# Low parts of the w_up weights: a ScalarE negation and an accumulating DMA in place of a VectorE subtraction

## The chip, the cores and the metric

The kernel runs on one core of one Trainium2 chip. The metric is the time of one execution on the device in microseconds (us); the profile gives the start and duration of every instruction of one such execution.

## What is computed

Two encoder layers on 512 positions of width 1024, all in float32. Cut to what matters here, a layer is

```python
h   = _mixer_sublayer(x, ...)                  # projections, two attention mixers, gates, w_out
x   = _layer_norm(DEEPNORM_ALPHA * x + h, ln1_g[i], ln1_b[i])
mlp = square(relu(x @ w_up[i])) @ w_down[i]    # 1024 -> 4096 -> 1024
ple = sigmoid(x @ w_ple_gate[i] + b_ple_gate[i]) * (p[i] @ w_ple[i])
x   = _layer_norm(DEEPNORM_ALPHA * x + mlp + ple, ln2_g[i], ln2_b[i])
```

The change concerns the weights `w_up` of the MLP.

## The kernel before

Every product of two float32 operands is made of three matmuls: each operand is split into a high part (rounded to the type float32r) and a low part (what is left), and the kernel sums high·high, low·high and high·low (`mm3`, lines 270 to 273). Weights come from HBM in packed sets of 128x1024 elements (512 KB). A set passes through three tiles, each with three buffers: `wst` (the raw weights, loaded by SP in `fetch`), `whi` and `wlo` (made in `prep` by the helper `split`). The helper is two instructions: ScalarE copies with a rounding, VectorE subtracts.

```python
nc.scalar.copy(hi, src)                                               # L225
nc.vector.tensor_tensor(lo, src, hi.bitcast(F32), ALU.subtract)       # L226
```

`weights(key, look, further)` hands out the next set and, before that, lets `ahead` prepare sets up to `look` places further on and fetch up to `further` places. With three buffers, set c+2 takes the buffers of set c-1, so its copy may begin when the product of set c-1 has ended.

The MLP of a layer goes in four quarters q of 1024 hidden channels. A quarter has an up stage and a down stage. The up stage is a loop over eight sets of `w_up`, in the order `UP_ORDER` (m = 0, 4, 1, 5, ...); the text below counts them by the loop index i, as P0 to P7 for their products. Each product is 24 matmuls (`mm3` for eight k) into one PSUM bank of the pool "mm". After each, `dn.hidden` writes the squared ReLU: ScalarE takes `r` (relu, L1016) and the high part (`a11h` L1020 for m < 4, `axh` L1023 otherwise), GpSimd takes `hr` = r·r (L1024), VectorE the low part (L1027, L1029). For m of 4 and more VectorE also forms four combinations `sr` (L1031 to L1033), which ScalarE copies to `smh` (L1034) and VectorE subtracts to `sml` (L1035).

The down stage multiplies these with `w_down` in seven products n of a Strassen-like scheme (`dn.product`, L1051), whose results VectorE adds to `yt` (`gather`, L1070). The sets of `w_down` lie in tiles `raw`; `dn.add` (L1004) sums two of them, and `dn.cut(q, n, c)` splits one by the same helper: the half c = 0 into the pool of `whi` and `wlo`, the half c = 1 into tiles `dhi` and `dlo`. So `w_up` sets and halves of `w_down` share three pairs of buffers. In each quarter the first cuts and adds are issued in the up loop, after P2 and later, and the first sets of the next quarter are prepared in the down stage (`behind`).

TensorE's order of work is the program's own (a manual schedule). On ScalarE, VectorE and GpSimd a scheduler with a time estimate of its own sets the order of the instructions, which the engines then run strictly in that order.

Of the kernel before, what the change touches and what calls it, by code (L numbers as in the profile page):

```python
# [10 lines left out]
F32 = mybir.dt.float32  # L11
F32R = mybir.dt.float32r
I32 = mybir.dt.int32
AF = mybir.ActivationFunctionType
ALU = mybir.AluOpType
# [185 lines left out]
def build(nc, tc, plan, down, xT, pT, wst, vec, sink, cst, outT):  # L201
# [3 lines left out]
    with ctx:  # L205
# [4 lines left out]
        def bank(tag, name):  # L210
            return pp.tile([P, 512], F32, tag=tag, name=name, bufs={"mm": 3, "s": 2, "pt": 2, "o": 1}[tag])
# [12 lines left out]
        def split(hi, lo, src):  # L224
            nc.scalar.copy(hi, src)  # L225
            nc.vector.tensor_tensor(lo, src, hi.bitcast(F32), ALU.subtract)  # L226
# [16 lines left out]
        def prep(c):  # L243
            st, n, cut = fetched.pop(c)
            hi = wp.tile([P, 1024], F32R, tag="whi", name=f"whi{c}")
            lo = wp.tile([P, 1024], F32R, tag="wlo", name=f"wlo{c}")
            for a in range(0, n, cut):
                split(hi[:, a:a + cut], lo[:, a:a + cut], st[:, a:a + cut])
            ready[c] = (hi, lo)

        def ahead(last, further=0):
            while at[1] < len(plan) and at[1] <= max(last, further):
                fetch(at[1])
                at[1] += 1
                if at[1] - 1 <= last:
                    prep(at[2])
                    at[2] += 1
            while at[2] < len(plan) and at[2] <= last:
                prep(at[2])
                at[2] += 1  # L260

        def weights(key, look=LOOK, further=0):
            c = at[0]
            assert plan[c][0] == key, (plan[c][0], key)
            at[0] += 1
            ahead(c + look, c + further)
            return ready.pop(c)

        def mm3(ps, w, i, x, start, stop):
            s = slice(i * P, (i + 1) * P)  # L270
            nc.tensor.matmul(ps, w[0][:, s], x[0], start=start, stop=False)  # L271
            nc.tensor.matmul(ps, w[0][:, s], x[1], start=False, stop=False)  # L272
            nc.tensor.matmul(ps, w[1][:, s], x[0], start=False, stop=stop)  # L273

        def linear(key, xs, ps=None):
            w = weights(key)
            if ps is None:
                ps = bank("mm", "ps_" + "_".join(str(v) for v in key))
            for i, x in enumerate(xs):
                mm3(ps, w, i, x, i == 0, i == len(xs) - 1)  # L280
            return ps
# [527 lines left out]
        class Norm:  # L809
# [87 lines left out]
            def behind(self, ins):  # L897
                tc.add_manual_dep(ins.ins, self.last.ins.name, mybir.DependencyInfo(
                    mybir.DependencyClass.Sync, mybir.DependencyReason.DATA), reason="statistics first")
# [245 lines left out]
        def pool(name, side="left"):  # L1145
            c = ExitStack()
            return c.enter_context(tc.tile_pool(name=name, bufs=1, side=side, reuse_waits="tile")), c.close
# [3 lines left out]
        for l in range(DEPTH):  # L1151
# [50 lines left out]
            for u in range(4):  # L1202
                gs = [gate(l, 1, t, vt, rp) for t in (2 * u, 2 * u + 1)]
                w = weights((l, ("bb", u)))
# [45 lines left out]
            def residual_turned(a):  # L1250
                for d in range(2):
                    tp = bank(("pt", "s")[a % 2], f"yT{l}_{a}_{d}")
                    for i in range(4):
                        nc.tensor.transpose(tp[:, i * P:(i + 1) * P], y[4 * d + i][:, a * P:(a + 1) * P], ident)
                    nc.scalar.copy(dn.y[a][:, d * 512:(d + 1) * 512], tp)
# [3 lines left out]
            with tc.manual_schedule(engines={PE}):  # L1259
                pss = []  # L1260
                for i in range(2):
                    pss.append(linear((l, ("up", 0, UP_ORDER[i])), X))
                    residual_turned(2 * i)
                    residual_turned(2 * i + 1)
                yp_close()
                p0_close()
                hp, hp_close = pool(f"hp{l}", "right")
                dn.hp = hp
                dn.operands()
                for q in range(FQ):  # L1270
                    for i, m in enumerate(UP_ORDER):
                        if not i:
                            dn.load(q)
                        if q or i > 1:
                            w = weights((l, ("up", q, m)), (2, 2, 2, 2, 2, 1, 1, 0)[i], min(3, 7 - i))
                            ps = bank("mm", f"ps_up{l}_{q}_{m}")
                            for k, x in enumerate(X):
                                mm3(ps, w, k, x, k == 0, k == KT - 1)
                        else:
                            ps = pss[i]  # L1280
                        dn.hidden(q, m, ps)
                        if i == 2:
                            dn.cut(q, 0, 1)
                        if q == FQ - 1 and i in (1, 2):
                            dn.spread(i - 1, dn.v[i - 1])
                        if i == 3:
                            dn.add(2, 1)
                            dn.cut(q, 1, 1)
                        if i == 4:
                            dn.add(5, 1)  # L1290
                        if i == 5:
                            dn.cut(q, 0, 0)
                        if i == 6:
                            dn.add(2, 0)
                            dn.add(5, 0)
                            dn.cut(q, 2, 1)
                        if i == 7:
                            dn.cut(q, 1, 0)
                            dn.add(3, 1)
                            dn.cut(q, 3, 1)  # L1300
                            dn.add(6, 1)
                    def behind(n, s):

                        with tc.issue_after(dn.ready.ins):
                            if n < 4:
                                if s:
                                    dn.cut(q, n + 2, 0)
                                    if n in (0, 1):
                                        dn.add((3, 6)[n], 0)
                                elif n:  # L1310
                                    dn.cut(q, n + 3, 1)
                            elif n == 4:
                                if not s:
                                    dn.cut(q, 6, 0)
                            elif s:
                                ahead(at[0] + n - 5, at[0] + 2)
                        if q == FQ - 1 and n == 1:
                            dn.moments(s, 0)

                    for n in range(7 if q < FQ - 1 else 4):  # L1320
                        dn.product(q, n, lambda s: behind(n, s))
                if not last:
                    ph, pl = (qp.tile([P, 2, S], F32R, name=f"p{e}{l + 1}", tag=f"raw11{i}", bufs=1) for i, e in enumerate("hl"))
                    pf = qp.tile([P, 2, S], F32, name=f"pf{l + 1}", tag="raw100", bufs=1)
                    nc.sync.dma_start(pf, pT[l + 1])
            q = FQ - 1
# [78 lines left out]
```

## Time and profile before

| | |
|---|---|
| three runs | 1571.17, 1571.31, 1573.22 us (median 1571.31) |
| the profiled execution, its own time | 1573.54 us |
| its span, first to last instruction | 1571.8 us |
| busy share of TensorE / VectorE / ScalarE / GpSimd | 98% / 69% / 47% / 18% |
| granted TensorE clock, mean | 0.996 of full speed |
| bytes moved, rate over the span | 143.37 MB, 91 GB/s |

The span lies 1.7 us under the execution's own time. A matmul's bar in the profile lasts longer than the distance to the next matmul's start, since matmuls overlap: rates are read from starts. A row of idle time names the instruction that ended it.

### The profile page before, as it was taken

To read this page: it belongs to the slowest core of one execution; us is meant where nothing else is said; L and a number is where in the kernel's file an instruction comes from. 1 tells how busy PE (TensorE), PEld (TensorE's weight loads), DVE (VectorE), ACT (ScalarE), POOL (GpSimd) and SP (SyncE) were. 2 spreads that over 40 slices of the span, in tenths; PEclk is the share of its full clock that TensorE was granted. 3 is DMA by queue.
4 is the path that set the end of the run, shared out by engine and by line. 5 is a ranking of instruction groups with operands and counts; after the bars stand their busy time and mean duration, and the time that the engine had idled before them with its cause. 6 is when DMAs were issued, how large, how long until landed. Compare 5 with 4: busy or idle time off the path is not lost.

```text
span 1571.8 us, 19688 instructions
## 1 busy us (share of the span) xinstructions
PE 1533.4 (98%) x7482; PEld 1254.0 (80%) x7482; DVE 1079.9 (69%) x1759; ACT 741.6 (47%) x1237; POOL 288.4 (18%) x208
## 2 busy tenths in 40 slices
PE   8999999999999999999899999999999999999997
PEld 6777888878888888888677778888887888888886
DVE  6878674454947777686868786744549476777867
ACT  4666554333644443434445665543336444434343
POOL 1010100157111111202000101101572111112020
PEclk9999999999999999999999999999999999999999
DMA  6212122232532414141132112223325324241401
GB/s 216 68 54 67 55 82 85 90 104 77 221 94 69 132 56 151 49 148 41 40 106 68 54 57 66 78 79 99 95 79 206 103 75 128 65 149 46 142 1 54
DMA packets 42736, 143.37 MB, mean 91 GB/s; under 512 B 5136, under 2 KB 7312, under 8 KB 42640
## 3 DMA queue, kind: packets, MB, share of 16 engines
q1 hardware_dynamic: 42064, 142.03, 28.4%
q8 instruction: 59, 0.97, 0.3%
q14 instruction: 37, 0.30, 0.1%
q10 hardware_dynamic: 576, 0.07, 0.0%
HBM read 139.98 MB, written 2.10 MB: 90 GB/s over the span
## 4 chain that ended last, share of the span: by engine, by line
PE 86%; DVE 8%; ACT 3%; issue 2%; DMA 1%; SPq 0%; ACTq 0%; DVEq 0%
PE dn L1051 16%; PE ps_up L273 7%; PE ps_up L272 7%; PE ps_up L271 7%; DVE wlo L226 2%; PE sa L399 1%; PE pta L377 1%; PE ps_start L271 1%; PE ps_start L272 1%; PE sb L399 1%; PE ps_start L273 1%; PE ya L271 1%; PE ya L273 1%; PE ya L272 1%; PE ps_pg L272 1%
## 5 line engine op out<-in xcount | busy, mean ns | idle before, releaser
L226 DVE TENSOR_TENSOR wlo<-wst,whi 128x1024 fp32r<-128x1024 f32 (+1 forms) x197 | 261.7, 1332 | 184.6 <-ACT whi L225 167.8
L225 ACT CAST whi<-wst 128x1024 fp32r<-128x1024 f32 (+1 forms) x197 | 202.3, 1029 | 352.8 <-PE ps_up L272 106.7
L1024 POOL TENSOR_TENSOR hr<-r 128x512 f32<-128x512 f32 x64 | 102.1, 1595 | 568.5 <-ACT r L1016 568.5
L271 PE MATMUL ps_up<-xhi,whi 128*128 128x512 f32 x480 | 186.9, 389 | 0.0
L273 PE MATMUL ps_up<-xhi,wlo 128*128 128x512 f32 x480 | 186.7, 389 | 0.0
L272 PE MATMUL ps_up<-xlo,whi 128*128 128x512 f32 x480 | 186.7, 389 | 0.0
L225 ACT CAST whi<-raw 128x1024 fp32r<-128x1024 f32 x56 | 58.0, 1052 | 101.4 <-PE ps_up L272 62.0
L272 PEld LDWEIGHTS ps_up<-xlo,whi 128*128 128x128 f32 x480 | 90.1, 188 | 18.8
L271 PEld LDWEIGHTS ps_up<-xhi,whi 128*128 128x128 f32 x480 | 90.1, 188 | 18.7
L273 PEld LDWEIGHTS ps_up<-xhi,wlo 128*128 128x128 f32 x480 | 90.1, 188 | 18.5
L225 ACT CAST dhi<-raw 128x1024 fp32r<-128x1024 f32 x56 | 58.8, 1052 | 82.8 <-PE dn L1051 59.5
L1070 DVE TENSOR_TENSOR yt<-yt,dn 128x512 f32<-128x512 f32 x96 | 65.3, 682 | 43.4 <-PE dn L1051 43.4
L1004 DVE TENSOR_TENSOR raw<-raw,raw 128x1024 f32<-128x1024 f32 x64 | 86.4, 1350 | 0.9 <-DMA raw<-wst 0.7
L226 DVE TENSOR_TENSOR wlo<-raw,whi 128x1024 fp32r<-128x1024 f32 x56 | 68.2, 1221 | 17.8 <-ACT whi L225 17.8
L226 DVE TENSOR_TENSOR dlo<-raw,dhi 128x1024 fp32r<-128x1024 f32 x56 | 68.2, 1220 | 5.1 <-ACT dhi L225 5.1
L336 POOL TENSOR_TENSOR sw_qb<-sw_qb,ct 128x512 f32<-128x512 f32 x12 | 18.4, 1536 | 181.9 <-DVE sw_qb L334 181.9
L1051 PE MATMUL dn<-whi,smh 128*128 128x512 f32 x128 | 50.1, 394 | 0.7 <-DVE yt L1070 0.7
L1051 PE MATMUL dn<-wlo,smh 128*128 128x512 f32 x128 | 50.6, 395 | 0.2
L1211 POOL TENSOR_TENSOR gate<-gate,gate 128x512 f32<-128x512 f32 x16 | 25.0, 1585 | 140.2 <-DVE gate L1210 140.2
L1051 PE MATMUL dn<-whi,sml 128*128 128x512 f32 x128 | 49.9, 390 | 0.0
L1051 PE MATMUL dn<-dhi,smh 128*128 128x512 f32 x128 | 49.9, 389 | 0.0
L1051 PE MATMUL dn<-dlo,smh 128*128 128x512 f32 x128 | 49.8, 389 | 0.0
(1015 smaller groups left out, 4048.0 us busy)
## 6 DMA issues: line engine op xcount, KB each, us to landing
wst<-wst SPq DMA_DIRECT2D x187, 512.0 KB, 3.6
raw<-wst SPq DMA_DIRECT2D x64, 512.0 KB, 4.4
wst<-wst SPq DMA_DIRECT2D x10, 256.0 KB, 2.7
xs<-xT SPq DMA_DIRECT2D x8, 256.0 KB, 4.7
outT<-nt SPq DMA_DIRECT2D x8, 256.0 KB, 2.2
ct<-cst SPq DMA_DIRECT2D x2, 960.0 KB, 8.0
pf<-pT SPq DMA_DIRECT2D x4, 256.0 KB, 4.0
pf<-pT SPq DMA_DIRECT2D x1, 512.0 KB, 3.5
```

Of the source, the lines that this page charges most:

```text
L225: nc.scalar.copy(hi, src)
L226: nc.vector.tensor_tensor(lo, src, hi.bitcast(F32), ALU.subtract)
L271: nc.tensor.matmul(ps, w[0][:, s], x[0], start=start, stop=False)
L272: nc.tensor.matmul(ps, w[0][:, s], x[1], start=False, stop=False)
L273: nc.tensor.matmul(ps, w[1][:, s], x[0], start=False, stop=stop)
L336: nc.gpsimd.tensor_tensor(sw, sw, cc["sin"], ALU.mult)
L399: nc.tensor.matmul(ss[r][:, col], q[a][rs, qs], k[b][rs, ks], start=n == 0, stop=n == 2)
L1004: nc.vector.tensor_tensor(to, to, other, ALU.add)
L1024: nc.gpsimd.tensor_tensor(h.rearrange("p s t -> p (s t)"), r, r, ALU.mult)
L1051: nc.tensor.matmul(ps[s], a[:, k, tok], w[b][:, cols], start=first and not (k or m), stop=k == 3 and m == 2, skip_group_check=True)
L1070: return nc.vector.tensor_tensor(to, to, ps, ALU.subtract if n in (2, 4, 5) else ALU.add)
L1211: nc.gpsimd.tensor_tensor(g, g, ga[t], ALU.add)
```

## The change

For sets of `w_up`, and only for them, `prep` no longer calls `split`. ScalarE copies the raw set to the high part as before (it is line 248 then), writes the negated high part into the tile of the low part (line 249), and a DMA issued from GpSimd adds the raw set to that tile (line 250). The look-ahead at i = 5 becomes two sets instead of one, so the last set of a quarter is prepared one product earlier, and `dn.cut(q, 0, 0)` moves from i = 5 to i = 6.

```diff
             hi = wp.tile([P, 1024], F32R, tag="whi", name=f"whi{c}")
             lo = wp.tile([P, 1024], F32R, tag="wlo", name=f"wlo{c}")
-            for a in range(0, n, cut):
-                split(hi[:, a:a + cut], lo[:, a:a + cut], st[:, a:a + cut])
+            if plan[c][0][1][0] == "up":
+                nc.scalar.copy(hi, st)
+                nc.scalar.activation(lo, hi.bitcast(F32), AF.Copy, scale=-1.0)
+                nc.gpsimd.dma_start(lo, st, accum_op=ALU.add)
+            else:
+                for a in range(0, n, cut):
+                    split(hi[:, a:a + cut], lo[:, a:a + cut], st[:, a:a + cut])
             ready[c] = (hi, lo)
...
-                            w = weights((l, ("up", q, m)), (2, 2, 2, 2, 2, 1, 1, 0)[i], min(3, 7 - i))
+                            w = weights((l, ("up", q, m)), (2, 2, 2, 2, 2, 2, 1, 0)[i], min(3, 7 - i))
...
-                        if i == 5:
+                        if i == 6:
                             dn.cut(q, 0, 0)
-                        if i == 6:
                             dn.add(2, 0)
                             dn.add(5, 0)
                             dn.cut(q, 2, 1)
```

There are 64 such sets (two layers, four quarters, eight sets). VectorE's queue becomes 64 instructions shorter, ScalarE's and GpSimd's 64 longer each. The order on TensorE and on SP is the same as before.

On ScalarE, in the second quarter of the first layer, this is the order around P2 and P3 before. `whi_4774` and `whi_4815` are the high parts of the sets 4 and 5; `r_1_4` and `r_1_1` belong to P1 and P2.

```order
L225 CAST whi_4774<-wst_4730 128x1024
L1016 ACTIVATE r_1_4_4761<-ps_up_1_4_4736 128x512
L1023 ACTIVATE axh_4149<-r_1_4_4761 128x512
L225 CAST whi_4815<-wst_4772 128x1024
L1034 CAST smh_4147<-sr_1_0_4766 128x1024
L1016 ACTIVATE r_1_1_4803<-ps_up_1_1_4778 128x512
L1020 ACTIVATE a11h_4145<-r_1_1_4803 128x256
L225 CAST whi_4862<-wst_4813 128x1024
```

And this is the order of the same work in the change, where `whi_4786` and `whi_4828` are the sets 4 and 5, and the rows of line 249 write the negated high parts.

```order
L248 CAST whi_4786<-wst_4741 128x1024
L1021 ACTIVATE r_1_4_4773<-ps_up_1_4_4748 128x512
L249 ACTIVATE wlo_4787<-whi_4786 128x1024
L1028 ACTIVATE axh_4153<-r_1_4_4773 128x512
L1039 CAST smh_4151<-sr_1_0_4778 128x1024
L248 CAST whi_4828<-wst_4784 128x1024
L1021 ACTIVATE r_1_1_4816<-ps_up_1_1_4791 128x512
L249 ACTIVATE wlo_4829<-whi_4828 128x1024
L1025 ACTIVATE a11h_4149<-r_1_1_4816 128x256
L248 CAST whi_4876<-wst_4826 128x1024
```

The negation stands behind `r` in each step, and `smh` now stands ahead of the high part of set 5, no longer behind it.

On GpSimd, before, the same stage holds nothing but the squares.

```order
L1024 TENSOR_TENSOR hr_0_0_4169<-r_0_0_4167 128x512
L1024 TENSOR_TENSOR hr_0_0_4169<-r_0_4_4173 128x512
L1024 TENSOR_TENSOR hr_0_1_4219<-r_0_1_4217 128x512
L1024 TENSOR_TENSOR hr_0_1_4219<-r_0_5_4258 128x512
L1024 TENSOR_TENSOR hr_0_2_4307<-r_0_2_4305 128x512
```

In the change, for the second quarter, the DMA of a step stands behind the square of that step: `wlo_4744` to `wlo_4877` are the sets 3 to 6.

```order
L1029 TENSOR_TENSOR hr_1_0_4737<-r_1_0_4735 128x512
L250 DMA wlo_4744<-wst_4703 128x1024
L1029 TENSOR_TENSOR hr_1_0_4737<-r_1_4_4773 128x512
L250 DMA wlo_4787<-wst_4741 128x1024
L1029 TENSOR_TENSOR hr_1_1_4818<-r_1_1_4816 128x512
L250 DMA wlo_4829<-wst_4784 128x1024
L1029 TENSOR_TENSOR hr_1_1_4818<-r_1_5_4858 128x512
L250 DMA wlo_4877<-wst_4826 128x1024
```

So each accumulating DMA is issued after the negation of its set and after one more square.

## Rows read from the trace of the kernel before

**Rows 1.** The page, part 1: busy us (share of the span) and instructions of each engine.

```profile
PE 1533.4 (98%) x7482; PEld 1254.0 (80%) x7482; DVE 1079.9 (69%) x1759; ACT 741.6 (47%) x1237; POOL 288.4 (18%) x208
```

**Rows 2.** Stretches: us, busy of PE, PEld, DVE, ACT, POOL, then PEclk, DMA share, GB/s.

```profile
500.00:530.00 30.00, 29.50 (x129) 23.64 (x129) 24.62 (x26) 13.01 (x14) 0.00 (x0) 1.00 0.48 144
530.00:570.00 40.00, 40.00 (x178) 33.14 (x177) 24.72 (x30) 17.59 (x25) 11.76 (x7) 1.00 0.32 102
sum 320.00, PE 318.87 PEld 261.68 DVE 231.72 ACT 133.14 POOL 49.47; mean PE 39.86 PEld 32.71 DVE 28.97 ACT 16.64 POOL 6.18
```

**Rows 3.** Waits of PE in the MLP, layer one, then layer two: us, times, longest.

```profile
PE dn L1051 <- DVE yt L1070: 1.0, 3, 0.5
...
PE dn L1051 <- DVE yt L1070: 0.4, 1, 0.4
```

**Rows 4.** Groups by form, 450 to 850 us: busy, mean ns, idle before, releaser.

```profile
L226 DVE TENSOR_TENSOR wlo<-wst,whi 128x1024 fp32r<-128x1024 f32 x40 | 49.3, 1241 | 44.2 <-ACT whi L225 38.1 <-PE yT L1254 5.9
...
L225 ACT CAST whi<-wst 128x1024 fp32r<-128x1024 f32 x40 | 41.9, 1051 | 83.6 <-PE ps_up L272 53.4 <-PE dn L1051 12.9 <-PE ps_start L272 8.0
...
L1034 ACT CAST smh<-sr 128x1024 fp32r<-128x1024 f32 x16 | 16.8, 1051 | 0.8 <-DVE sr L1033 0.8
L1023 ACT ACTIVATE axh<-r 128x512 fp32r<-128x512 f32 x16 | 10.2, 635 | 0.5
...
L1024 POOL TENSOR_TENSOR hr<-r 128x512 f32<-128x512 f32 x31 | 49.5, 1596 | 239.0 <-ACT r L1016 239.0
```

**Rows 5.** Timeline of PE, P0 and the first matmul of P1, quarter two: start, duration.

```profile
526.14 0.39 PE L271 MATMUL ps_up<-xhi,whi 128*128 128x512 f32 x1
...
526.60 0.39 PE L273 MATMUL ps_up<-xhi,wlo 128*128 128x512 f32 x1
...
531.58 0.39 PE L271 MATMUL ps_up<-xhi,whi 128*128 128x512 f32 x1
```

**Rows 6.** Timeline of ACT in the same up stage, set 2 and sets 4 to 5.

```profile
525.03 1.05 ACT L225 CAST whi<-wst 128x1024 fp32r<-128x1024 f32 x1 [3.83 <-PE dn L1051]
...
537.00 1.05 ACT L225 CAST whi<-wst 128x1024 fp32r<-128x1024 f32 x1 [3.40 <-PE ps_up L272]
537.95 0.59 ACT L1016 ACTIVATE r<-ps_up 128x512 f32<-128x512 f32 x1
538.57 0.63 ACT L1023 ACTIVATE axh<-r 128x512 fp32r<-128x512 f32 x1
542.44 1.05 ACT L225 CAST whi<-wst 128x1024 fp32r<-128x1024 f32 x1 [3.23 <-PE ps_up L272]
543.39 1.05 ACT L1034 CAST smh<-sr 128x1024 fp32r<-128x1024 f32 x1
544.34 0.59 ACT L1016 ACTIVATE r<-ps_up 128x512 f32<-128x512 f32 x1
```

**Rows 7.** Timeline of POOL, the squares behind P1 and P2.

```profile
538.62 1.59 POOL L1024 TENSOR_TENSOR hr<-r 128x512 f32<-128x512 f32 x1 [3.81 <-ACT r L1016]
545.06 1.72 POOL L1024 TENSOR_TENSOR hr<-r 128x512 f32<-128x512 f32 x1 [4.85 <-ACT r L1016]
```

**Rows 8.** Timeline of DVE, the last of the combinations behind P1.

```profile
542.03 0.43 DVE L1033 SCALAR_TENSOR_TENSOR sr<-sr,hr 128x256 f32<-128x256 f32 x1
```

**Rows 9.** The page, part 6: DMA issues, KB each, median us from issue to landing.

```profile
wst<-wst SPq DMA_DIRECT2D x187, 512.0 KB, 3.6
...
wst<-wst SPq DMA_DIRECT2D x10, 256.0 KB, 2.7
...
ct<-cst SPq DMA_DIRECT2D x2, 960.0 KB, 8.0
```

**Rows 10.** Timeline of ACT, end of the first quarter's down stage.

```profile
514.48 1.04 ACT L225 CAST whi<-wst 128x1024 fp32r<-128x1024 f32 x1
515.42 1.04 ACT L225 CAST dhi<-raw 128x1024 fp32r<-128x1024 f32 x1
```

**Rows 11.** Timeline of DVE in the same stretch.

```profile
517.48 1.22 DVE L226 TENSOR_TENSOR dlo<-raw,dhi 128x1024 fp32r<-128x1024 f32 x1
518.61 1.22 DVE L1004 TENSOR_TENSOR raw<-raw,raw 128x1024 f32<-128x1024 f32 x1
519.75 1.28 DVE L1070 TENSOR_TENSOR yt<-yt,dn 128x512 f32<-128x512 f32 x2
```

## The prediction, made before the changed kernel was run

> **What bounds the kernel now.** I read the shares of the engines first: PE is busy for 98% of the span, DVE for 69%, ACT for 47%, POOL for 18% [rows 1]. A gain must therefore come out of time in which PE stands, in the stages that the change touches. The table of stretches shows how much that is: over an up stage (530 to 570 us) PE is busy 40.00 of 40.00 us, and over the whole MLP of the first layer (450 to 770 us) 318.87 of 320.00 us, at full granted clock [rows 2]. The waits name what is left: PE waits for DVE's `yt` in the down products, 1.0 us in the first layer and 0.4 us in the second, and for nothing in the up products [rows 3]. Last the timeline of PE gives the pace: P0 starts at 526.14 us, its third matmul, the first that reads `wlo`, at 526.60, and P1 at 531.58 [rows 5]. A product takes 5.44 us, and its low part is needed 0.46 us after its start. The MLP goes at the pace of the matmuls, and the change does not touch these.
>
> **The change, part by part.** *VectorE loses 64 subtractions.* One takes 1.24 us [rows 4], in all 79 us. But no up product waits for DVE, so the place to look is the down stage, where PE waits for `yt`. The longest of these waits is at 519.75 us, where `yt` starts late because DVE, which runs in order, is still in a subtraction `dlo` and an addition `raw` of 1.22 us each [rows 11]. Both stay; the subtractions for `w_up` sets stand behind them. So I count nothing. The bound for a gain is all of PE's idle time in the MLP: 320.00 - 318.87 = 1.1 us a layer [rows 2], 2.3 us for two.
>
> *ScalarE gains 64 negations.* The trace has no negation of 128x1024, but the copies of that size take 1.05 us [rows 4], so 67 us in all. In the fullest step of an up stage ACT then runs `whi` 1.05, `r` 0.59, the negation 1.05, `axh` 0.63 and `smh` 1.05 [rows 4, 6], together 4.4 us of the 5.44 of a product. ACT has the room; what counts is what stands behind the negation in its queue. `r` stands ahead of it, so PSUM banks come free as before. At the end of a down stage the negation of set 0 goes between `whi` at 514.48 and the `dhi` that ran at 515.42 [rows 10]. That `dhi` then ends near 517.6, and DVE's `dlo`, which started at 517.48 [rows 11], starts up to 0.2 us later, and with it the `yt` for which PE waits. This happens at six changes of quarter, at most 1.2 us; as the second layer has only 0.4 us of such waits [rows 3], and so more slack, I take 0.5 us.
>
> *The low part now arrives by a chain: ScalarE, GpSimd, DMA.* I follow the steps at P2 in the times of the trace. The high part of set 4 starts with P2 at 537.00, `r` at 537.95 [rows 6], the negation where `axh` stood, 538.57 to 539.6. On GpSimd the square runs from 538.62 to 540.21 [rows 7], and the DMA behind it goes out at 540.3. P4 starts at 537.0 + 2 x 5.44 = 547.9 and needs the low part at 548.36, so 8.1 us are left.
>
> Set 5 is worse off. `smh` now stands ahead of its copy. The combinations behind P1 end at 542.03 + 0.43 = 542.46 [rows 8], so `smh` starts at 542.5 where the copy of set 5 started at 542.44 [rows 6]; the copy follows 0.95 us later, at 543.45. `r` comes at 544.4 as before (544.34). The square on GpSimd runs from 545.1 for 1.72 us [rows 7], the negation is done by 546.1, and the DMA goes out at 546.85. P5 needs the low part at 531.58 + 4 x 5.44 + 0.46 = 553.8. **The DMA has 6.95 us** from its issue to its landing. Set 7 has the same position behind the next `smh`, sets 3 and 6 that of set 4. Set 2, whose copy ran at 525.03 [rows 6] and before which GpSimd is free, is negated by 527.1 and has 10.4 us.
>
> *How long the DMA takes* is the one number that the trace does not hold, since GpSimd issues none. From below: an SP load of 512 KB lands after 3.6 us [rows 9], if the addition costs nothing. From above: 960 KB, about the bytes of two sources, land after 8.0 us, and GpSimd might be occupied as long as by a square, 1.6 us [rows 4]: 9.6 us. Between: 256 KB land after 2.7 us, so 256 KB more cost 0.9 us and a second source of 512 KB 1.8 us, which makes 3.6 + 1.8 = 5.4 us; I add 0.5 us for GpSimd, near the low end, because the times of [rows 9] already hold an issue. I take 5.9 us, nearest to the loads of the same size and shape. That is 1 us inside the limit of 6.95, so the up stage stays covered and the term is zero. If a landing takes X us, set 5 is late by X - 6.95, and P5 and everything behind shifts by as much, which relieves set 7 of the same quarter. That is eight stalls, one in each quarter.
>
> By the Trainium skill (DMA: Bandwidth & Descriptors, Latency and other measured facts) a DMA through GpSimd starts its first byte about 1 us after issue, where one through SP takes about 0.6 us; as an estimate from that page the landing would be 5.4 + 0.4 = 5.8 us and the sum the same.
>
> *The raw sets are held longer.* Their buffers come free when the DMA has landed. Set 3 goes out 3.3 us after P1's start and lands 5.9 later, at 9.2; the load of set 6 takes 3.6 [rows 9], to 12.8, and its copy starts with P4, at 16.3. The cover is 3.5 us. What stands behind that load on SP is only needed in the next down stage.
>
> *Look-ahead and the moved cut.* Set 7 is made one product earlier and the first cut of the down stage one later. That cut now starts with P6, is a copy and a subtraction of 1.05 and 1.24 us [rows 4], and is needed 10.9 us later. Zero; if DVE were late here, the first down product would pay.
>
> **The sum.** 0 + 0.5 + 0 = +0.5 us. Against the profiled execution that is 1573.5 + 0.5 = 1574.0 us. That execution lies 2.2 us above the median of the runs shown, 1571.3, so for a median I give 1571.8 us.
>
> **The rivals.** *The DMA lands too late (slower).* It decides from 6.95 us on. With 8.0 us, the landing of 960 KB, set 5 of each quarter is late by 1.05 us: 8 x 1.05 = +8.4 us, 1580 us. With 9.6 us the sets 3, 5 and 7 are late by 9.6 - 8.1 = 1.5 us each, 4.6 us a quarter, +37 us, 1608 us. For it speaks that no row shows such a DMA and that the margin is only 1 us; against it that DMA engines are busy for only 0.32 of the up stage [rows 2], and that ACT, POOL and PE reach their times in the chain by rows of this trace.
>
> *GpSimd's issue is held up by VectorE (slower).* In this kernel it would wait for DVE instructions under way, two of 1.22 us [rows 11], so that the landing comes at 5.9 + 2.4 = 8.3 us: 1.35 late in set 5 and 0.2 in sets 3 and 7, 1.75 a quarter, +14 us, 1586 us. The Trainium skill (SBUF — State Buffer, Who interferes with whom) has GpSimd starved of descriptor generation while VectorE runs in a two-port mode, and exempts `tensor_tensor`. By that exemption the case is unlikely; DVE's work here is nearly all tensor-tensor subtraction at one speed, 1.22 to 1.24 us for 1024 elements [rows 4, 11], which fits it.
>
> *VectorE's relief reaches PE (faster).* If the freed DVE time ended every wait in the MLP, the time would be 1571.3 - 2.3 = 1569.0 us. Against it: the removed subtractions stand behind the late `yt`, and even this is within 0.2%.
>
> **How the numbers follow.** About 0.2%, 3.1 us, is what a measurement of this kernel can tell from no change. The forecast, no stall in the up stage, has a chance of 0.63; the late DMA 0.25; the held issue 0.07; a gain beyond 2.3 us or from a place that I do not see 0.05. So: faster 0.05, same 0.63, slower 0.32. The range begins at 1569.0, the bound of the gain. A late DMA of up to about 8.5 us costs 1.55 us in set 5 and 0.4 in the sets behind and ahead, some 16 us for eight quarters; I let the range reach 1588 and leave about 0.13 above it and 0.04 below.
>
> **What would show it.** Right: PE busy for 40 of 40 us in an up stage, no wait of PE for `wlo`, matmuls of products 5.44 us apart at the start; the DMA rows at 6.95 us or less from issue to landing; DVE's share down by 79 us, ACT's up by 67 us, both without effect on the span. Wrong: PE waiting at line 278 (273 before) for a DMA, first of all in P5, or a fresh wait in the down products for `yt`. A DMA of 8 us or more would make the forecast wrong, and so would a scheduler's order that holds `r` back until banks run out.

## The result, and the profile after

| comparison | before, us | change, us | ratio, with its 95% interval |
|---|---|---|---|
| the first (14 runs each) | 1572.57 | 1575.61 | 1.0018 [1.0009, 1.0026] |
| repeated beside experiments (11 against 21 runs) | 1573.04 | 1573.68 | 1.0002 [0.9994, 1.0011] |
| repeated once more (11 against 21 runs) | 1573.35 | 1575.22 | 1.0013 [1.0004, 1.0021] |

By the measure named ahead (0.2%) the change makes no difference. The three comparisons put it 0.6 to 3.0 us behind the kernel before, and two of the three intervals lie above 1; the forecast was +0.5 us.

Part 1 of the page of the changed kernel: VectorE 76.9 us less than in [rows 1], ScalarE 57.6 us more, GpSimd 24.7 us more, PE's share still 98%.

```profile
PE 1535.9 (98%) x7482; PEld 1255.3 (80%) x7482; DVE 1003.0 (64%) x1695; ACT 799.2 (51%) x1301; POOL 313.1 (20%) x272
```

The stretches that answer to [rows 2] (us, busy of PE, PEld, DVE, ACT, POOL, then PEclk, DMA share, GB/s): an up stage keeps PE busy for 40.00 of 40.00 us as before, with a DMA share of 0.74 where it was 0.32.

```profile
500.00:530.00 30.00, 29.30 (x128) 23.50 (x127) 22.39 (x24) 16.14 (x17) 2.59 (x3) 1.00 0.62 175
530.00:570.00 40.00, 40.00 (x178) 33.11 (x177) 17.39 (x24) 21.51 (x29) 12.20 (x12) 1.00 0.74 184
450.00:770.00 320.00, 318.67 (x1405) 261.35 (x1405) 196.46 (x244) 158.88 (x195) 59.76 (x60) 1.00 0.54 137
```

The groups that answer to [rows 4], from the page. The negation takes as long as the copy; the issue occupies GpSimd for 0.88 us; the square `hr`, 1.60 us before, takes 1.10.

```profile
L249 ACT ACTIVATE wlo<-whi 128x1024 fp32r<-128x1024 f32 x64 | 67.5, 1055 | 0.6
L250 POOL DMA_DIRECT2D wlo<-wst x64 | 56.3, 880 | 308.9 <-ACT wlo L249 206.1
L1029 POOL TENSOR_TENSOR hr<-r 128x512 f32<-128x512 f32 x64 | 70.5, 1102 | 237.5 <-ACT r L1021 194.4
```

The last line of the view of line 250:

```profile
DMA to landing us min/median/max: 4.5/5.9/8.4
```

PE waits for no `wlo` in the up stages. Its wait for `yt`, 1.4 us in [rows 3], is 2.3 us in this profile (1.8 and 1.7 us in those of the two repeats), and a small wait in the second layer's attention is new:

```profile
PE dn L1056 <- DVE yt L1075: 2.3, 5, 0.7
...
PE firstn L277 <- DVE alm L1219: 0.3, 1, 0.3
```

Set 5 of the second quarter of the first layer, the one that the prediction followed, reads so in the timeline of GpSimd, with the square behind P1 and the one behind P2:

```profile
539.79 1.03 POOL L1029 TENSOR_TENSOR hr<-r 128x512 f32<-128x512 f32 x1 [3.28 <-ACT r L1021]
...
545.61 1.03 POOL L1029 TENSOR_TENSOR hr<-r 128x512 f32<-128x512 f32 x1 [3.67 <-ACT r L1021]
546.82 0.88 POOL L250 DMA_DIRECT2D wlo<-wst  x1 [0.18 <-ACT a11h L1025]
```

In the DMA view of the stretch with that one issue (the last number is the time to landing, us):

```profile
wlo<-wst POOLq DMA_DIRECT2D x1, 512.0 KB, 6.9
```

And in the timeline of PE, where the first matmul of P5 to read its `wlo` is the one at 554.96:

```profile
554.50 0.39 PE L276 MATMUL ps_up<-xhi,whi 128*128 128x512 f32 x1
554.73 0.39 PE L277 MATMUL ps_up<-xlo,whi 128*128 128x512 f32 x1
554.96 0.39 PE L278 MATMUL ps_up<-xhi,wlo 128*128 128x512 f32 x1
```

So the DMA had 554.96 - 546.82 = 8.14 us and took 6.9. The forecast had 6.95 us and 5.9. The margin, 1.2 us, is about the forecast's, but both numbers behind it are larger.

I worked out the same three numbers for every set of the quarters 1 to 3, in the three profiles of the change (the times to need are those of most of them):

| set | time from issue to need, us | landings, us | least margin, us |
|---|---|---|---|
| 2 | 9.9 | 4.8 to 7.6 | 2.3 |
| 3 | 8.46 | 4.8 to 8.3 | 0.16 |
| 4 | 8.46 | 4.8 to 7.1 | 1.3 |
| 5 | 8.13 | 5.3 to 7.7 | 0.43 |
| 6 | 8.46 | 4.8 to 8.1 | 0.31 |
| 7 | 8.13 | 4.5 to 7.3 | 0.8 |

The thinnest margin is in the profile of the first repeat, in the third quarter of the first layer. Its issue on GpSimd, its landing, and the matmul of PE that needs it:

```profile
617.90 0.89 POOL L250 DMA_DIRECT2D wlo<-wst  x1 [0.17 <-ACT a11h L1025]
```

```profile
wlo<-wst POOLq DMA_DIRECT2D x1, 512.0 KB, 8.3
```

```profile
626.36 0.39 PE L278 MATMUL ps_up<-xhi,wlo 128*128 128x512 f32 x1
```

626.36 - 617.90 - 8.3 = 0.16 us. The up stage is covered, but by much less than the median landing lets one think. (In all 56 stops of PE in the three runs below with a late DMA, its matmul starts 0.04 us after the landing, so the landing is the time that counts.)

A second cover is as thin. The raw set of set 6 can only be loaded when the accumulating DMA of set 3 has landed and set free its buffer, and it must be there when ScalarE copies it at the start of P4. In the second quarter of the second layer the timeline of SP has the load, the DMA view its time to landing, and the timeline of ScalarE the copy:

```profile
1329.26 0.33 SPq L240 DMA_DIRECT2D wst<-wst  x1
```

```profile
wst<-wst SPq DMA_DIRECT2D x1, 512.0 KB, 6.9
```

```profile
1336.43 1.05 ACT L248 CAST whi<-wst 128x1024 fp32r<-128x1024 f32 x1 [2.32 <-PE ps_up L277]
```

The load lands 0.2 us before the copy (0.15 and 0.08 us in the profiles of the repeats). In four of the other quarters 1 to 3 set 6 has 1.1 to 1.6 us, in the last quarter of the second layer 4.6 us or more.

### The profile page after: what moved, and what is told of

Its sections match the earlier page's. It is cut to its first block, busy times and chain, and to the rows that moved or that the text cites. A ratio compares the mean times of both kernels' runs of the same rounds, so it can differ in the third digit from the quotient of the medians.

```text
span 1574.7 us, 19942 instructions
## 1 busy us (share of the span) xinstructions
PE 1535.9 (98%) x7482; PEld 1255.3 (80%) x7482; DVE 1003.0 (64%) x1695; ACT 799.2 (51%) x1301; POOL 313.1 (20%) x272
## 4 chain that ended last, share of the span: by engine, by line
PE 86%; DVE 8%; ACT 3%; issue 2%; DMA 1%; SPq 0%; ACTq 0%; DVEq 0%
PE dn L1056 15%; PE ps_up L277 7%; PE ps_up L276 7%; PE ps_up L278 7%; DVE wlo L226 2%; PE sa L404 1%; PE sb L404 1%; PE pta L382 1%; PE ya L276 1%; PE ya L278 1%; PE ya L277 1%; PE ps_pg L277 1%; DMA raw<-wst 1%; PE ps_pg L278 1%; PE ps_start L277 1%
## 5 line engine op out<-in xcount | busy, mean ns | idle before, releaser
L226 DVE TENSOR_TENSOR wlo<-wst,whi 128x1024 fp32r<-128x1024 f32 (+1 forms) x133 | 184.3, 1387 | 113.0 <-ACT whi L225 108.2
L225 ACT CAST whi<-wst 128x1024 fp32r<-128x1024 f32 (+1 forms) x133 | 134.9, 1017 | 176.8 <-PE ya L277 19.7
L248 ACT CAST whi<-wst 128x1024 fp32r<-128x1024 f32 x64 | 67.3, 1051 | 111.1 <-PE ps_up L277 58.0
L1029 POOL TENSOR_TENSOR hr<-r 128x512 f32<-128x512 f32 x64 | 70.5, 1102 | 237.5 <-ACT r L1021 194.4
L250 POOL DMA_DIRECT2D wlo<-wst x64 | 56.3, 880 | 308.9 <-ACT wlo L249 206.1
L1036 DVE TENSOR_TENSOR sr<-hr 128x512 f32<-128x512 f32 x32 | 22.0, 687 | 89.9 <-POOL hr L1029 89.9
L249 ACT ACTIVATE wlo<-whi 128x1024 fp32r<-128x1024 f32 x64 | 67.5, 1055 | 0.6
L1040 DVE TENSOR_TENSOR sml<-sr,smh 128x1024 fp32r<-128x1024 f32 x32 | 39.2, 1225 | 35.9 <-ACT smh L1039 35.9
```

Of the source, the lines that this page charges most:

```text
L248: nc.scalar.copy(hi, st)
L249: nc.scalar.activation(lo, hi.bitcast(F32), AF.Copy, scale=-1.0)
L250: nc.gpsimd.dma_start(lo, st, accum_op=ALU.add)
L1029: nc.gpsimd.tensor_tensor(h.rearrange("p s t -> p (s t)"), r, r, ALU.mult)
```

## The experiments

**Sets 0 to 2 by VectorE again** (in the quarters 1 to 3; no negation is then left in front of `dhi` at the changes of quarter).

```diff
-            if plan[c][0][1][0] == "up":
+            key = plan[c][0][1]
+            if key[0] == "up" and not (key[1] and UP_ORDER.index(key[2]) < 3):
```

> The change, but the sets 0 to 2 of the quarters 1 to 3 (18 of 64, those prepared in a down stage) get their low part by VectorE's subtraction again, so no negation stands ahead of dhi there. Theory A (the up stage is covered, and what the change costs lies at the change of quarter, where the negation holds dhi back, and with it VectorE's dlo and yt, for which TensorE waits): TensorE's waits for yt in the down products fall from 2.3 us over both layers to about 1.4, as before, and the time is some 1.3 us under the change (1.0000 to 1.0015 of before). Theory B (the accumulating DMAs load the DMA queues or the issue through GpSimd slows something else throughout): the waits do not matter and the time stays within 1 us of the change (1.0015 to 1.0025), since 46 of 64 DMAs remain.

Measured: 1573.09 us, ratio 1.0001 [0.9992, 1.0009]; PE's wait for `yt` is back at 1.4 us; that proves little by itself, since the repeats of the change have 1.8 and 1.7 us. The time is that of the kernel before, as far as the interval tells.

```profile
PE dn L1057 <- DVE yt L1076: 1.4, 4, 0.4
```

**The look-ahead and the moved cut alone**, with the low parts made by VectorE everywhere.

```diff
-            if plan[c][0][1][0] == "up":
-                nc.scalar.copy(hi, st)
-                nc.scalar.activation(lo, hi.bitcast(F32), AF.Copy, scale=-1.0)
-                nc.gpsimd.dma_start(lo, st, accum_op=ALU.add)
-            else:
-                for a in range(0, n, cut):
-                    split(hi[:, a:a + cut], lo[:, a:a + cut], st[:, a:a + cut])
+            for a in range(0, n, cut):
+                split(hi[:, a:a + cut], lo[:, a:a + cut], st[:, a:a + cut])
```

> The longer look-ahead and the moved cut alone; all low parts by VectorE as before. Theory A: nothing hangs on either, 0.9990 to 1.0010 of before, TensorE's waits for yt 1.4 us as before. If the moved cut is what costs, 1.001 to 1.003 with new waits in the first two down products.

Measured: 1572.98 us, ratio 1.0004 [0.9995, 1.0013], with a wait for `yt` of 1.9 us. By themselves these two edits cost or gain nothing that this comparison can tell.

**The change with the old look-ahead**, where set 7 is made one product later.

```diff
-    (2, 2, 2, 2, 2, 2, 1, 0)[i]
+    (2, 2, 2, 2, 2, 1, 1, 0)[i]
...
-                        if i == 6:
+                        if i == 5:
                             dn.cut(q, 0, 0)
+                        if i == 6:
```

> The change without the longer look-ahead and with the cut at i = 5 as before, so set 7 of each quarter is prepared only from the start of P6 on. Theory A: its DMA goes out 2.9 us after P6 starts, lands 4.5 to 5.9 us later, and P7 needs it 5.9 us after the start of P6: TensorE stands 1.5 to 2.9 us at line 278 in each of eight P7, 12 to 23 us in all, 1.008 to 1.015 of before, and the only new wait is this one. Theory B would have the stalls spread over the sets; and if a DMA took much less than its landing time says, there would be no stall.

Measured: 1587.99 us, ratio 1.0096 [1.0081, 1.0112], +15 us over the kernel before. PE now waits for the DMA eight times, once in each P7, by 1.6 us each by the starts of its matmuls, 12.8 us in all. By these starts there is a ninth stop, of 0.3 us, in P5 of the third quarter of the second layer, where set 5 took 8.4 us to land. The row of PE's waits, then, for the second quarter of the first layer, the timelines of GpSimd and of PE:

```profile
PE ps_up L278 <- DMA wlo<-wst: 11.5, 8, 1.5
```

```profile
563.55 0.89 POOL L250 DMA_DIRECT2D wlo<-wst  x1 [0.24 <-issue]
```

```profile
566.35 0.39 PE L277 MATMUL ps_up<-xlo,whi 128*128 128x512 f32 x1
568.15 0.50 PE L278 MATMUL ps_up<-xhi,wlo 128*128 128x512 f32 x1 [1.41 <-DMA wlo<-wst]
```

The issue is at 563.55, PE is ready for `wlo` at 566.58 (566.35 and the spacing of 0.23) and gets it at 568.15: 4.6 us, near the shortest landing of 4.5. This is the late DMA of the rivals, in set 7 in place of set 5, and it shows what the longer look-ahead is there for in this design.

**A plain copy in place of the accumulation** (the raw set overwrites the negated high part).

```diff
-                nc.gpsimd.dma_start(lo, st, accum_op=ALU.add)
+                nc.gpsimd.dma_start(lo, st)
```

> The DMA through GpSimd copies the raw set into the low part's tile instead of adding it (this leaves out the addition). It measures what the second source costs. As the prediction's sum has it, 1.8 us: landing 4.1 us instead of 5.9. If the issue through GpSimd is the cost, the landing stays at 5.5 us or more. The time stays within 0.1% of the change under theory A, since nothing waits for the landing in either; under theory B it falls towards before, as a third of these bytes is gone.

Measured: 1574.09 us, ratio 1.0012 [1.0003, 1.0021]; PE's wait for `yt` is 1.8 us. The landings fall from 5.9 to 3.0 us, and GpSimd is busy for 0.58 us per issue, where it was 0.88 (the view of line 250, and the groups of GpSimd).

```profile
DMA to landing us min/median/max: 2.9/3.0/5.8
```

```profile
L250 POOL DMA_DIRECT2D wlo<-wst x64 | 37.0, 579 | 311.7 <-ACT wlo L249 230.9 <-DVE yt L1075 34.7 <-DVE y L1246 30.0
```

Half the DMA time saves nothing: it was hidden. The second source costs 5.9 - 3.0 = 2.9 us in the median and 4.5 - 2.9 = 1.6 us in the shortest landings. The plain copy also loads the DMA engines less, so how much of the 2.9 us is the load is not told apart.

**Six small additions in front of the DMA** of the sets 3 to 7.

```diff
                 nc.scalar.activation(lo, hi.bitcast(F32), AF.Copy, scale=-1.0)
+                if UP_ORDER.index(plan[c][0][1][2]) > 2:
+                    for _ in range(6):
+                        nc.gpsimd.tensor_tensor(rgap, lo[:, :80].bitcast(F32), lo[:, :80].bitcast(F32), ALU.add)
                 nc.gpsimd.dma_start(lo, st, accum_op=ALU.add)
```

> The change, but in front of the DMA of the sets 3 to 7 of every quarter GpSimd does six small additions (128x80 into a scratch tile) that wait for the negation. They delay the issue; nothing else moves. Going by the square of 128x512 at 1.10 us, one of 80 columns is some 0.2 to 0.3 us, six are 1.2 to 1.8 us. Theory A (the up stage has a margin of about 2.2 us in set 5, 8.1 us from issue to need against a landing of 5.9): delayed by less than that, the time stays that of the change, 1575 to 1577 us, with no wait of PE for wlo in P5. Theory B (the margin is 1 us, as forecast from the trace of before, 6.95 - 5.9): stalls of 0.2 to 0.8 us for set 5 or 7 in each quarter, +2 to +7 us over the change.

Measured: 1592.06 us, ratio 1.0123 [1.0104, 1.0142]. Both numbers were missed, because the additions delay the DMA by more than I had estimated. The timeline of GpSimd, for set 4 and set 5, and PE's wait:

```profile
544.41 3.08 POOL L252 TENSOR_TENSOR rgap<-wlo 128x80 f32<-128x80 f32 x6
547.90 0.89 POOL L253 DMA_DIRECT2D wlo<-wst  x1 [0.41 <-POOL rgap L252]
...
550.54 2.45 POOL L252 TENSOR_TENSOR rgap<-wlo 128x80 f32<-128x80 f32 x6
553.40 0.88 POOL L253 DMA_DIRECT2D wlo<-wst  x1 [0.41 <-POOL rgap L252]
```

```profile
PE ps_up L281 <- DMA wlo<-wst: 11.8, 11, 2.1
```

Six cost 2.4 to 3.1 us, and the DMA starts 0.4 us behind them: some 3 us, more than either theory's margin, so this run does not decide between 2.2 and 1 us. The sets 4 and 5 then have 5.2 us in a quarter without an earlier stop, and every landing over that stops PE. The recorded waits are 11.8 us; by the starts of the matmuls the stops and the slower first matmul behind each are some 16 us. Another 1.6 us come from the clock: behind the stop of 2.3 us at 471.5 the granted clock is 0.72 in the next 6 us (matmuls 0.43 us apart, the 1.2 GHz level, for a part of it), where the change itself has 1.00. The scheduler also put one `smh` in each of six quarters behind the next copy and `r`, so not only the DMA moved.

```profile
465.00:473.00 8.00, 6.89 (x31) 5.36 (x29) 3.36 (x5) 4.90 (x6) 5.81 (x11) 1.00 0.65 134
473.00:479.00 6.00, 5.01 (x15) 3.99 (x16) 0.71 (x2) 1.95 (x4) 3.96 (x8) 0.72 0.92 219
```

**Eight small additions**, with which the scheduler also puts the DMA of set 5 and set 7 behind the next square.

> The same with eight small additions. The scheduler now puts the DMA of the sets 5 and 7 behind the square of the next product. For set 5 that square starts with r of P3, 5.44 us after r of P2 (544.88 in the second quarter of the changed kernel): 550.3 + 0.6 + 1.1 = 552.0, so the DMA goes out near 552.1 and the low part is needed at 554.96. Theory A (what counts is issue plus landing, 5.9 us, against the need): 3.0 us late in set 5, and again in set 7, since its square follows the shifted product: 8 x 2 x 3.0 = +48 us over the change, 1620 us, and PE's waits for DMA wlo in P5 and P7 alone. Theory B (the landing has hidden slack, for PE reads wlo column by column, or the DMA lands sooner with less beside it, 4.5 us): 1.6 us or less each, under +26 us.

Measured: 1615.01 us, ratio 1.0267 [1.0253, 1.0281], +39.4 us over the change in the first comparison and +41.3 us over that in this one. The sum is nearer A's, the pattern is neither's: PE waits 30 times, by 0.9 us on the average, in P4 to P7. Most single stops have B's size (by the starts of the matmuls 28 of 32 are 1.6 us or less), but there are twice as many as either theory counted.

```profile
PE ps_up L281 <- DMA wlo<-wst: 26.5, 30, 3.0
```

Eight additions take 3.2 to 4.4 us, so set 4 is late already; and a DMA for which PE waits lands in 4.5 to 5 us mostly, not in 5.9, as B had it.

**Set 0 alone by VectorE** (quarters 1 to 3), twice, each time beside the change itself. The order moves elsewhere too: in four of these six quarters SP loads one raw set ahead of a `w_up` set, and some of the work on ScalarE and VectorE changes places.

```diff
-            if plan[c][0][1][0] == "up":
+            key = plan[c][0][1]
+            if key[0] == "up" and not (key[1] and UP_ORDER.index(key[2]) < 1):
```

> The change, but set 0 of the quarters 1 to 3 of each layer (6 of 64) is made by VectorE's subtraction again; this is the one set whose negation stands ahead of dhi at a change of quarter. Theory A (the whole cost of the change is that negation, in front of dhi, dlo and the yt for which PE waits): the time of the kernel with the sets 0 to 2 made by VectorE, 1573.1 us, ratio 1.000 to 1.0005, and PE's wait for yt back from 2.3 to 1.4 us. Theory B (the cost lies in the sets 1 and 2 too, or is spread over the up stages, start and clock): more than 1574.3 us, half of the cost or more is left, ratio 1.001 or more.

> The change itself once more, beside the others on the same chip. Theory A and B alike: ratio 1.0018 with its interval of 1.0009 to 1.0026, 1575.0 to 1576.3 us for a kernel before of 1572.5; it tells by how much e7 is below the change on the same chip. Should it come out at 1.0005 or less, the cost of the change is not reproduced and its cause can't be told from these runs.

> The change itself a third time. The first comparison gave a ratio of 1.0018, the second 1.0002. Theory A (the change costs the +0.5 to +1.2 us at the changes of quarter and nothing else; the rest of the first ratio belonged to that comparison): 1.0000 to 1.0008. Theory B (the first ratio is the typical one): 1.0014 or more.

> Set 0 of the quarters 1 to 3 by VectorE once more, in the same comparison. Theory A (the cost is the negation in front of dhi): under the change of this comparison by 0.5 to 1.2 us, as it was by 1.2 us in the one before, ratio 0.9995 to 1.0003. Theory B (set 0 plays no part, and 1.2 us was chance): equal to the change within 0.3 us, or above it.

Measured: 1572.45 us (0.9998 [0.9989, 1.0007]) beside 1573.68 for the change (1.0002), then 1573.42 us (1.0007 [0.9998, 1.0016]) beside 1575.22 (1.0013). The variant lies 1.2 and 1.8 us under the change. The intervals against the kernel before overlap, but run against run the change is the slower in 79% and 82% of all pairs, so the times go A's way. The profiles do not support A's mechanism: the recorded waits for `yt` are 1.7 and 2.3 us in the variant, 1.8 and 1.7 in the change. The first repeat of the change, 1.0002, lies under the 1.0005 at which I had said that its cause can't be told; the second, 1.0013, lies between the ranges of the two theories.

What the wait for `yt` hangs on is seen at the first change of quarter of the first layer. First ScalarE in the change, then in the first run with set 0 on VectorE:

```profile
514.59 1.05 ACT L225 CAST dhi<-raw 128x1024 fp32r<-128x1024 f32 x1 [1.87 <-DMA raw<-wst]
515.55 1.05 ACT L248 CAST whi<-wst 128x1024 fp32r<-128x1024 f32 x1
516.63 1.06 ACT L249 ACTIVATE wlo<-whi 128x1024 fp32r<-128x1024 f32 x1
517.60 1.04 ACT L225 CAST dhi<-raw 128x1024 fp32r<-128x1024 f32 x1
```

```profile
513.04 1.05 ACT L225 CAST dhi<-raw 128x1024 fp32r<-128x1024 f32 x1 [1.51 <-DMA raw<-wst]
513.99 1.05 ACT L225 CAST whi<-wst 128x1024 fp32r<-128x1024 f32 x1
514.94 1.04 ACT L225 CAST dhi<-raw 128x1024 fp32r<-128x1024 f32 x1
```

The negation does stand in front of the second `dhi` and pushes it by 1.1 us (517.60 - 515.55 = 2.05 us behind the copy, where it was 0.95). But the wait is set by the first `dhi`, which waits for a raw set to land. I measured, in nine profiles, its start after the first matmul of the down stage, and the gap that PE then has at `axh` beyond the usual spacing (first layer, first change of quarter):

| profile | start of that `dhi`, us | gap of PE, us |
|---|---|---|
| before | 26.62 | 0.62 |
| look-ahead alone | 26.68 | 0.68 |
| sets 0 to 2 by VectorE | 26.46 | 0.47 |
| set 0 by VectorE, two runs | 26.39, 26.78 | 0.36, 0.78 |
| the change, three runs | 26.73, 26.66, 26.50 | 0.85, 0.76, 0.59 |
| plain copy | 26.58 | 0.70 |

The gap is the start less 26.0 us without the negation, less 25.9 us with it. The negation costs 0.1 us here; the rest is when the raw set lands, which varies by 0.4 us between the two runs of one kernel (26.39 and 26.78). The same reading of the other five changes of quarter gives 0.1 us at three of them and nothing at the third change of either layer, and no gap where the `dhi` starts early. So the negation costs 0.4 us at most in an execution.

The sums of the gaps say less. Over all six changes they are 0.96 to 2.08 us without the negation (mean of five profiles 1.5) and 1.49 to 2.35 with it (mean of four 1.9). This +0.4 us is no larger than the standard deviation within either group (0.4), and the three profiles with a late DMA, which have the negation too, show 0.97, 1.65 and 2.25.

## Why the prediction was right, and where its steps were off

**The up stage stays covered: right.** PE is busy for 40.00 of 40.00 us and waits for no `wlo` in three profiles of the change. VectorE's 77 us and ScalarE's 58 us (67.5 of negations, whose bars overlap that of each neighbour by 0.1 us) leave no mark on the span, as forecast.

**The limit of 6.95 us: mis-sized.** The step that went wrong is the length of two squares, 1.59 and 1.72 us in [rows 7]; both took 1.03. Beside the one behind P1 ran a subtraction that the change removes (538.08); beside the one behind P2 ran `sml`, which stood behind another such subtraction. The timeline of VectorE before, and `sml` in the change, which now ends before that square starts (545.61):

```profile
538.08 1.23 DVE L226 TENSOR_TENSOR wlo<-wst,whi 128x1024 fp32r<-128x1024 f32 x1 [2.81 <-ACT whi L225]
...
543.52 1.23 DVE L226 TENSOR_TENSOR wlo<-wst,whi 128x1024 fp32r<-128x1024 f32 x1 [1.07 <-ACT whi L225]
544.67 1.22 DVE L1035 TENSOR_TENSOR sml<-sr,smh 128x1024 fp32r<-128x1024 f32 x1
```

```profile
544.06 1.23 DVE L1040 TENSOR_TENSOR sml<-sr,smh 128x1024 fp32r<-128x1024 f32 x1 [1.12 <-ACT smh L1039]
```

The square behind P1 ends sooner, so the combinations, `smh`, the copy of set 5 and `r` come 0.67 us sooner, counted from P1; the one behind P2 is shorter by another 0.7. Less 0.15 us between its end and the issue, the DMA goes out 1.2 us earlier, and the low part has 8.13 us.

**The landing of 5.9 us: right as a median, wrong as what decides.** Two errors met in it, and that they cancel is luck. I took 3.6 us and 0.5 for GpSimd for one source, and 1.8 for the second; the plain copy shows 3.0 and 2.9. And a margin has to hold against the longest landing, not the median: landings reach 8.3 us in the up stages, whose DMA share is 0.74. (The 8.4 us of the view is set 1 of a quarter, which has 10.9 us.) In the first profile of the change five of the sixteen landings of the sets 5 and 7 were over 6.95 us (7.1, 7.1, 7.3, 7.3, 7.7). Had the limit been what I took it for, these would have stalled PE by 0.15 to 0.75 us each. The forecast held because for the sets 5 and 7 of the quarters 1 to 3 the limit was too short by 1.2 us and the longest landing by 1.8: of the forecast margin of 1.05 us, 0.43 were left. That both errors went the same way is luck too.

**The raw sets held longer: zero, but not with the cover forecast.** I gave the load of set 6 a cover of 3.5 us; it was 1.1 to 1.6 us in most quarters and 0.08 to 0.24 us in one. Beside the accumulating DMAs that load took 3.6 to 7.2 us (3.4 to 4.6 in the profile of before), not the 3.6 of [rows 9], and the landing of set 3 before it was longer than 5.9 us in most quarters. No run here delays this load by itself, so what a late one would cost is not shown.

**Look-ahead and the moved cut: zero, as forecast** (1.0004 [0.9995, 1.0013] by themselves).

**The late DMA (rival, 0.25): did not come, but it was near**, by 0.16 us in one quarter. The run with the old look-ahead and the two with additions show it at +15, +19 and +42 us over the kernel before of the same comparison, with a row of PE waiting for `wlo` each time. My price for it, the time by which the landing misses, holds for the stops of up to 2.0 us, behind which the granted clock stayed at 1.00; behind those of 2.2, 2.3 and 3.2 us it was 0.72 in the next 6 us, which cost another 1.6 us or so each. Two of my prices are a little dear by my own rule that a stop relieves the sets behind it: for landings of 8.3 and 9.6 us a late set 3 relieves set 5, which makes 1.55 and 4.15 us a quarter in place of 1.75 and 4.6.

**The held issue (rival, 0.07): not seen.** The 64 issues occupied GpSimd for 0.85 to 1.01 us each, beside VectorE's subtractions (in the first profile 0.85 to 0.89 us for the 17 beside its work on 128x1024) as away from them. That agrees with the exemption of `tensor_tensor` in the Trainium skill (SBUF — State Buffer, Who interferes with whom). The estimate by the Trainium skill (DMA: Bandwidth & Descriptors, Latency and other measured facts), 5.8 us, met the median landing; its reason, a later start through GpSimd, is not seen apart from the rest, as the plain copy through GpSimd took 3.0 us and SP's loads, which come from HBM, 3.6.

**The negation ahead of `dhi`, +0.5 us: right in size.** It is 0.1 us at four of the six changes of quarter, 0.4 us at most. What I had not seen is that the length of the wait is set by the `dhi` before it, which waits for its raw set, and so varies between executions by as much as this term.

**What the measured +0.6 to +3.0 us is made of** is known in part: 0.4 us at most there, and 0.3 us of a new wait for `alm`. That wait stands in all three profiles of the change, in the plain copy's and in the old look-ahead's, but in neither of the two with additions, which have all the negations as well, and in none with set 0 or all sets by VectorE; its cause stays open. The MLP of both layers together, from the first up matmul to the last down matmul, takes 636.6 us in the profile of before and 637.7, 637.4 and 636.7 in those of the change; with set 0 or all sets by VectorE it takes 636.7 to 637.7 as well. The rest lies in stages without a changed instruction, and comes in steps of 1 to 1.6 us, most of them with the granted clock, which differ between executions of one kernel as well. In the stretch 775 to 805 us, the start of the second layer, the granted clock was 0.89 before, 0.89 in the first profile of the change and 0.77 in that of the first repeat; in the stretch 1175 to 1200 us, in which PE stands for 2.7 us, it was 1.00, 0.93 and 1.00. The rows in this order:

```profile
775.00:805.00 30.00, 22.92 (x93) 17.68 (x92) 22.86 (x51) 20.21 (x36) 0.00 (x0) 0.89 0.31 104
1175.00:1200.00 25.00, 22.34 (x99) 17.45 (x98) 23.52 (x27) 16.92 (x24) 11.62 (x7) 1.00 0.60 223
```

```profile
775.00:805.00 30.00, 22.56 (x96) 17.36 (x94) 22.04 (x50) 21.52 (x38) 0.00 (x0) 0.89 0.31 103
1175.00:1200.00 25.00, 22.31 (x92) 17.27 (x91) 23.01 (x34) 16.27 (x24) 11.64 (x7) 0.93 0.56 213
```

```profile
775.00:805.00 30.00, 23.84 (x87) 18.09 (x86) 21.54 (x49) 20.85 (x37) 0.00 (x0) 0.77 0.29 103
1175.00:1200.00 25.00, 22.32 (x101) 17.57 (x101) 23.62 (x36) 16.60 (x24) 11.63 (x7) 1.00 0.55 208
```

Whether the change makes such stretches more frequent, and why set 0 on VectorE should make them rarer, is not settled by these runs. No variant was faster than the kernel before.

## What to carry to other kernels

Relieving an engine of 77 us bought nothing here, where another engine is at 98% and waits for none of that work: look first for a wait that the removed instruction ends. When a DMA replaces a short instruction on a chain with a due time, compare the time left with the longest landing under the load that the change itself creates, not with the median, and look at each set, since positions in the order differ. Do the same for the loads that wait for the buffers which that DMA holds. And work out the time left again with the changed neighbours: here GpSimd's squares became shorter when VectorE's subtractions of `w_up` sets were gone.

## What was not expected of the hardware

- GpSimd's square of 128x512 went from 1.60 to 1.10 us, though nothing in it was changed. In the profile of before the 8 squares of 64 without a tensor-tensor instruction of VectorE beside them take 1.04 us, the 56 others 1.53 to 1.88; in the change 56 take 1.03 or 1.04 us and 8, with VectorE beside them, 1.58. Of the eight in the stretch 520 to 575 us most take 1.03 or 1.04 us; the one that still takes 1.58 runs beside subtractions and additions of VectorE on 128x1024, and one of those additions, 1.22 us elsewhere, takes 1.95 there. That they hinder each other is read from where they stand, not tried by itself. The timelines of GpSimd and of VectorE in the changed kernel:

```profile
561.55 1.58 POOL L1029 TENSOR_TENSOR hr<-r 128x512 f32<-128x512 f32 x1 [2.96 <-ACT r L1021]
```

```profile
561.00 1.23 DVE L226 TENSOR_TENSOR wlo<-raw,whi 128x1024 fp32r<-128x1024 f32 x1 [2.88 <-ACT whi L225]
562.26 1.95 DVE L1009 TENSOR_TENSOR raw<-raw,raw 128x1024 f32<-128x1024 f32 x1
```

- Accumulating doubles the median landing of a 512 KB move from tile to tile: 3.0 us without and 5.9 with it; the shortest are 2.9 and 4.5 us.
- Small additions on GpSimd are dear: one of 80 columns starts 0.40 us after the one before it (the median in a row of six), where a square of 512 columns takes 1.03.
